# One 512-column product for both halves of the activations in the q, k and z projections

## The chip, the cores and the metric

The kernel runs on one core of a Trainium2 chip. The metric is the time of one execution on the device in microseconds (us); lower is better. TensorE (PE) multiplies, ScalarE (ACT) and VectorE (DVE) work on what it returns and on the weights, SyncE's queue (SP) issues nearly all loads.

## What is computed

Two decoder layers on 256 tokens of width 2048, in float32. Each layer normalises, scales and shifts its input, projects it, runs an attention, gates with silu(z), projects back and adds to the residual. Layer A has a dilated mixer with three patterns, so its projection makes ten parts of 2048 columns (q, k and v three times, and z); layer B has block attention and four parts (q, k, v, z). A last norm follows.

```
for i in range(DEPTH):                                    # DEPTH = 2
    mod = cond @ mod_w[i] + mod_b[i]
    shift, scale, gate = jnp.split(mod[:, None, :], 3, axis=-1)
    h = rms_norm(x, norm_w[i]) * (1.0 + scale) + shift
    if i % N_MIXERS == 0:
        y = dilated_mixer(h, a_w_in[j], slopes) @ a_w_out[j]
    else:
        y = moba_mixer(h, b_w_in[j], slopes) @ b_w_out[j]
    x = x + gate * y
return rms_norm(x, final_norm_w)
```

## The kernel before

**Split operands.** Every float32 operand of the big products is split into a high part that float32r holds exactly and a low part, the rest. A product is three passes: high by high, low by high, high by low. The activations lie split in SBUF as `hA` (layer A) and `hB` (layer B), tiles of 128 rows, 16 chunks, 2 halves (high, low) and 256 tokens, so the two halves of one chunk lie side by side, 512 columns in all.

**Units of weights.** A unit is 256 rows by 512 columns of a weight matrix, 512 KB. `convert` (L353) asks SP for its load into one of five buffers `raw`, and ACT copies it to the high part `wh` (L362); `finish_converts` (L366) lets DVE make the low part `wl` (L369). There are four buffers of `wh` and `wl` (`NB`, a ring); eight units held for longer use others.

**Parts and steps.** The sixteen heads are worked in four groups `j` of four heads. A part is one of q, k, v, z for one group: 8 units, 512 columns. Weights of v parts move past standing activations (`moving`, L303, products of 512 columns into two accumulators of 128 tokens). For q, k and z the weights stand and activations move (`stationary`, L315): for a head and a chunk of 128 rows three products of 256 columns, `wh` by high, `wh` by low, `wl` by high, all into the same 256 columns. Two heads share one PSUM bank, so a part takes two of the four accumulators `acc`, and the next part takes the other two. `evac` (L551) copies the finished banks to SBUF on ACT, with Silu for z.

**Order.** The order is written out by hand. A step is the products of one unit; `steps` lists them. `at_once(i, f)` puts work right after step i's products and ahead of the splitting of the next weights; `at(i, f)` puts it behind. `plan_conversions` (L372) lets a unit be loaded and split after the step in which the unit four places ahead in the ring was last used, and not over 8 steps ahead. Each engine works through its own instructions in that order.

**Stages.** Layer A begins with group 0 and six parts of group 1 (v0, v1, v2, z, q0, k0) in five strips of rows, since the modulation's scale and shift come strip by strip; each strip's products are added to what the earlier ones left (`evac_partial`, L542, on DVE). The last strip is one unit wide: 16 steps. Then come q1, k1, q2, k2 of group 1, all ten parts of group 2 and of group 3, the output projection, layer B's four groups (v, z, q, k), its output projection and the last norm. The attention of a group runs as items (`item_a`, one head and half the queries, 8 in a group; `item_b`, one head, 4 in a group), whose four stages are hung on later steps with given offsets: scores, normalising, transposes, output. Group 0's items begin at steps i0, i0 + 1, ... of group 1's q1, where i0 is the first step behind the strips. `add_piece` spreads loads of the modulation's weights and DVE's multiply-adds on them (L136) evenly over the steps of layer A behind the strips, and over layer B's groups 1 and 2.

Of the kernel before, what the change touches and what calls it, by code (L numbers as in the profile page):

```python
# [11 lines left out]
F32 = mybir.dt.float32  # L12
# [5 lines left out]
P = 128  # L18
# [13 lines left out]
def distance_masks():  # L32
    """-(t_q - t_k) where a key is seen, MASKED elsewhere, in blocks of 128 queries by 128 keys.

    The first six blocks: tokens of one parity each; the last three: tokens of one half each.
    """
    m = np.arange(P)

    def block(tq, tk, rule):
        d = tq[:, None] - tk[None, :]  # L40
        return np.where(rule(d), -d.astype(np.float32), np.float32(MASKED)).astype(np.float32)

    near = lambda d: (d >= 0) & (d <= 128)
    every = lambda n: (lambda d: (d >= 0) & (d % n == 0))
    even, odd, low, high = 2 * m, 2 * m + 1, m, m + P
    cols = [block(even, even, near), block(even, odd, near), block(even, even, every(4)), block(even, even, every(16)),
            block(odd, even, near), block(odd, odd, near)]
    cols += [block(q, k, lambda d: d >= 0) for q, k in ((low, low), (high, low), (high, high))]
    return np.ascontiguousarray(np.concatenate(cols, axis=1))
# [3 lines left out]
def trunk_kernel(ctx: ExitStack, tc: tile.TileContext, x, c, norm_w, mod_w, mod_b, a_w_in, a_w_out,  # L53
# [25 lines left out]

# [1 line left out]
    xnT = [ypool.tile([P, 8, S], F32, name=f"xnT{i}", tag=f"y{i}") for i in range(2)]  # L81
# [36 lines left out]

# [1 line left out]
    slots = {}  # L120

    def slot(i, name, dtype=F32):
        """A new tile in slot i, 0 .. 15."""
        if i < 12:
            return actp.tile([P, 1024], dtype, name=name, tag=f"a{i}")
        y = 2 + (i - 12) // 2
        if i % 2 == 0:
            slots[y] = ypool.tile([P, 2048], F32, name=f"ext{y}", tag=f"y{y}")
        return slots[y][:, (i % 2) * 1024:(i % 2 + 1) * 1024]

# [1 line left out]
    def mac(acc, raw, kc, first):  # L132
# [12 lines left out]
    def start_unit(u):  # L145
        """Strip 0: four chunks of rows of scale (u < 4) or shift; part of shift on the tensor engine."""
        part, i = 1 - u // 4, u % 4
        raw = rawp.tile([P, 4, 256], F32, name="raw", tag="raw")
        src = mod_w[0, i * 512:(i + 1) * 512, part * D:part * D + 256]
        nc.sync.dma_start(raw, src.rearrange("(c p) n -> p c n", p=P))  # L150
        for k in range(4):
            kc = 4 * i + k
            if u < 4 or 4 <= kc < 14:
                mac(start_acc[:, part * 256:(part + 1) * 256], raw[:, k], kc, (u, k) in ((0, 0), (5, 0)))
                continue
            for b in range(2):
                nc.tensor.matmul(start_ps[:, b:b + 1], raw[:, k, b * P:(b + 1) * P], ccT[:, kc:kc + 1],
                                 start=u == 4 and k == 0 and b == 0, stop=False, skip_group_check=True)
# [6 lines left out]
    def strip_unit(s, u):  # L165
        """Loads 1024 weights a partition of strip s of layer 0's shift (first half of the units) or scale."""
        w = 256 * STRIPS[s]
        n = 1024 // w
        part, i = divmod(u, KC // n)
        if u == 0:  # L170
            strip_acc[s] = maccp.tile([P, 1024], F32, name="macc", tag="macc")
        raw = rawp.tile([P, n, w], F32, name="raw", tag="raw")
        n0 = part * D + sum(STRIPS[:s]) * 256
        nc.sync.dma_start(raw, mod_w[0, i * n * P:(i + 1) * n * P, n0:n0 + w].rearrange("(c p) n -> p c n", p=P))
        for k in range(n):
            mac(strip_acc[s][:, part * w:(part + 1) * w], raw[:, k], i * n + k, i == 0 and k == 0)
# [13 lines left out]
    def column_sums(sums, acc, g, pool, tag):  # L190
        """sums[:, g] := sums over the rows of acc's columns 512 g .., 128 to a column."""
        pc = pool.tile([P, 512], F32, name="pcs", tag=tag)
        for b in range(4):
            nc.tensor.transpose(pc[:, b * P:(b + 1) * P], acc[:, (4 * g + b) * P:(4 * g + b + 1) * P], ident)
        nc.vector.tensor_reduce(sums[:, 4 * g:4 * g + 4], pc.rearrange("p (b k) -> p b k", b=4), axis=AX.X, op=ALU.add)
# [39 lines left out]

# [1 line left out]
    def rstd_of(ss, n):  # L237
        """(ss / D + EPS) ** -0.5"""
        r = small.tile([P, 2], F32, name="rstd")
        nc.gpsimd.tensor_scalar(r[:, :n], ss, 1.0 / D, EPS, op0=ALU.mult, op1=ALU.add)  # L240
        nc.gpsimd.tensor_tensor(r[:, :n], r[:, :n], nhalf[:, :n], op=ALU.pow)
        return r

    def split(dst, src):
        """dst[p, k, 0 / 1, t] := high and low part of src[p, k, t]."""
        hi = dst[:, :, 0]
        nc.scalar.activation(hi, src, AF.Copy)
        nc.vector.tensor_tensor(dst[:, :, 1], src, hi.bitcast(F32), op=ALU.subtract)
# [52 lines left out]

# [1 line left out]
    def moving(ps, st, kcs, w, tts, first, last):  # L303
        """ps[token, tile, n] += st.T @ w, for two chunks of rows of w."""
        wh, wl = w
# [9 lines left out]
    def stationary(ps, st, kcs, w, first, last):  # L315
        """ps[n, head, token] += w.T @ st"""
        wh, wl = w
# [9 lines left out]

# [1 line left out]
    units, steps, tasks, first_tasks, conv = [], [], {}, {}, {}  # L329
# [5 lines left out]

    def add_step(n, pe):
        i = len(steps)
        steps.append((n, pe))
        if units[n]["first"] is None:
            units[n]["first"] = i  # L340
        units[n]["last"] = i
        return i
# [4 lines left out]
    def at_once(i, f, *a):  # L347
        """As at, but ahead of the splitting of the next weights."""
        first_tasks.setdefault(i, []).append((f, a))
# [3 lines left out]
    def convert(n):  # L353
        """Loads a unit and makes its high parts; finish_converts() the low ones."""
        raw = rawp.tile([P, 2, GC], F32, name="raw", tag="raw")
# [16 lines left out]
    def plan_conversions():  # L372
        """After which step each unit is loaded and split: its tiles are free then."""
        ring, held, e, plan = [], {}, -1, {}
# [17 lines left out]

# [1 line left out]
    act = {}  # L394
# [18 lines left out]
    def bias_exp(ps, dmc, slope, parts, t):  # L413
        """t := exp of scaled scores with their bias, less the rows' maxima, in parts of columns; their sums."""
        n, w = len(parts), parts[-1].stop
# [24 lines left out]
    def item_a(j, hh, tt, base, offsets):  # L440
        """One head and one tile of queries of the dilated mixer."""
        st = {}
# [37 lines left out]
    def item_b(j, hh, base, offsets):  # L480
        """One head of the block mixer (one block): the queries of the first half see its keys, the others all."""
        st = {}
# [30 lines left out]

# [1 line left out]
    PARTS = ["v0", "v1", "v2", "z", "q0", "k0", "q1", "k1", "q2", "k2"]  # L515
# [17 lines left out]
    def product(p, key, st, n, u, first, last):  # L533
        def pe():
# [3 lines left out]
            else:  # L538
                moving(group_ps(key), st, kcs, conv[n], (0, 1), first, last)
        return add_step(n, pe)  # L540

    def evac_partial(key, s):  # L542
# [38 lines left out]
    for j in range(1, 4):  # L581
        i0 = len(steps)
        for i in range(8):
            base = i0 + i if j == 1 else i0 + 1 + 2 * i
            item_a(j - 1, i // 2, i % 2, base, (0, 1, 2, 4) if j == 1 else (0, 1, 3, 5))
        for n, p in enumerate(PARTS[EARLY:] if j == 1 else PARTS):
            for u in range(8):
                m = add_unit(wA, u, COL[p] * D + j * GC)
                i = product(p, ("A", j, p), st_a, m, u, u == 0, u == 7)
            at_once(i + 6 if j == 1 and n == 0 else i, evac, "A", j, p)  # L590

# [6 lines left out]

# [1 line left out]
    def out_steps(l, w, epilogue, hold):  # L600
# [102 lines left out]

# [1 line left out]
    st_b = lambda kc: hB_box[0][:, kc]  # L705
    for j in range(4):
# [4 lines left out]
        for p in PARTS_B:  # L711
            col = COL_B[p] * D + j * GC
            if j == 0 and p == "v":
                ns = [add_unit(wB, u, col, HOLD[u] if u < 4 else None)
                      for u in range(8)]
                for tt in range(2):
                    for u, n in enumerate(ns):
                        def pe(n=n, u=u, tt=tt, key=("B", j, p)):
                            moving(group_ps(key), st_b, (2 * u, 2 * u + 1), conv[n], (tt,), u == 0, u == 7)
                        i = add_step(n, pe)  # L720
            else:
                for u in range(8):
# [40 lines left out]

# [1 line left out]
    plan = plan_conversions()  # L765
# [55 lines left out]
```

## Time and profile before

| what | value |
|---|---|
| median of 3 runs | 1614.94 us (1614.93 to 1617.24) |
| span of the profiled execution | 1612.8 us |
| time of the profiled execution | not given apart from its span; the median is 2.1 us above the span |
| TensorE busy | 1579.9 us, 98% |
| TensorE weight loads busy | 1478.9 us, 92% |
| DVE busy | 1136.5 us, 70% |
| ACT busy | 743.6 us, 46% |

The span runs from the first to the last instruction that the profile shows. Products are pipelined and their ends are modelled, so TensorE's busy share says little of how much of its time is needed; weight loads run beside the products.

### The profile page before, as it was taken

To read this page: it belongs to the slowest core of one execution; us is meant where nothing else is said; L and a number is where in the kernel's file an instruction comes from. 1 tells how busy PE (TensorE), PEld (TensorE's weight loads), DVE (VectorE), ACT (ScalarE), POOL (GpSimd) and SP (SyncE) were. 2 spreads that over 40 slices of the span, in tenths; PEclk is the share of its full clock that TensorE was granted. 3 is DMA by queue.
4 is the path that set the end of the run, shared out by engine and by line. 5 is a ranking of instruction groups with operands and counts; after the bars stand their busy time and mean duration, and the time that the engine had idled before them with its cause. 6 is when DMAs were issued, how large, how long until landed. Compare 5 with 4: busy or idle time off the path is not lost.

```text
span 1612.8 us, 27220 instructions
## 1 busy us (share of the span) xinstructions
PE 1579.9 (98%) x10975; PEld 1478.9 (92%) x10975; DVE 1136.5 (70%) x1477; ACT 743.6 (46%) x971; POOL 12.1 (1%) x29
## 2 busy tenths in 40 slices
PE   5999999999999999999999999999999999999997
PEld 4999999999999889999889999887998999989986
DVE  6899899888756876666876665766446767664565
ACT  4643434334544544444544443554445445454543
POOL 0000000000000000000000000000000000000000
PEclk9999999999999999999999999999999999999999
DMA  9988797766468779888778887466467787856553
GB/s 310 322 280 293 247 322 263 253 208 185 133 205 272 230 238 298 282 285 278 232 261 286 280 287 233 126 210 211 133 183 237 253 267 239 278 166 202 172 170 119
DMA packets 182253, 380.97 MB, mean 236 GB/s; under 512 B 11616, under 2 KB 19952, under 8 KB 181616
## 3 DMA queue, kind: packets, MB, share of 16 engines
q1 hardware_dynamic: 180352, 373.93, 71.6%
q0 software_dynamic: 1008, 4.19, 0.7%
q8 instruction: 86, 1.41, 0.3%
q10 hardware_dynamic: 768, 1.12, 0.2%
q14 instruction: 39, 0.32, 0.1%
HBM read 377.10 MB, written 2.10 MB: 235 GB/s over the span
## 4 chain that ended last, share of the span: by engine, by line
PE 94%; DMA 2%; DVE 2%; ACT 1%; issue 1%; POOL 0%; POOLq 0%; DVEq 0%; ACTq 0%
PE acc L326 18%; PE acc L325 18%; PE acc L324 18%; PE acc L311 11%; PE acc L313 10%; PE acc L312 10%; PE po L472 2%; PE pss L454 2%; DMA raw<-in_mod_w_dram 2%; PE pst L435 1%; PE po L505 1%; PE pss L489 1%; DVE macc L136 1%; DMA raw<-in_a_w_in_dram 1%; ACT wh L362 0%
## 5 line engine op out<-in xcount | busy, mean ns | idle before, releaser
L362 ACT ACTIVATE wh<-raw 128x1024 fp32r<-128x1024 f32 x504 | 533.1, 1059 | 672.6 <-PE acc L325 396.3
L369 DVE TENSOR_TENSOR wl<-raw,wh 128x1024 fp32r<-128x1024 f32 (+1 forms) x505 | 612.8, 1220 | 261.5 <-ACT wh L362 260.3
L324 PE MATMUL acc<-hA,wh 128*128 128x256 f32 x1792 | 509.4, 284 | 0.0
L326 PE MATMUL acc<-hA,wl 128*128 128x256 f32 x1792 | 507.1, 283 | 0.0
L325 PE MATMUL acc<-hA,wh 128*128 128x256 f32 x1792 | 507.0, 283 | 0.0
L325 PEld LDWEIGHTS acc<-hA,wh 128*128 128x128 f32 x1792 | 343.9, 192 | 0.7
L324 PEld LDWEIGHTS acc<-hA,wh 128*128 128x128 f32 x1792 | 343.8, 192 | 0.7
L326 PEld LDWEIGHTS acc<-hA,wl 128*128 128x128 f32 x1792 | 343.8, 192 | 0.0
L136 DVE SCALAR_TENSOR_TENSOR macc<-raw,ccT,macc 128x1024 f32<-128x1024 f32 (+2 forms) x264 | 247.2, 936 | 22.8 <-DMA raw<-in_mod_w_dram 19.1
L324 PE MATMUL acc<-hB,wh 128*128 128x256 f32 x768 | 219.8, 286 | 0.0
L326 PE MATMUL acc<-hB,wl 128*128 128x256 f32 x768 | 217.4, 283 | 0.0
L325 PE MATMUL acc<-hB,wh 128*128 128x256 f32 x768 | 217.3, 283 | 0.0
L311 PE MATMUL acc<-wh,hA 128*128 128x512 f32 x384 | 155.4, 405 | 3.7 <-ACT actA1v L547 1.4
L312 PE MATMUL acc<-wl,hA 128*128 128x512 f32 x384 | 151.0, 393 | 0.3 <-DVE wl L369 0.3
L313 PE MATMUL acc<-wh,hA 128*128 128x512 f32 x384 | 150.8, 393 | 0.0
L324 PEld LDWEIGHTS acc<-hB,wh 128*128 128x128 f32 x768 | 147.3, 192 | 0.3
L325 PEld LDWEIGHTS acc<-hB,wh 128*128 128x128 f32 x768 | 147.3, 192 | 0.3
L326 PEld LDWEIGHTS acc<-hB,wl 128*128 128x128 f32 x768 | 147.2, 192 | 0.0
L311 PEld LDWEIGHTS acc<-wh,hA 128*128 128x128 f32 x384 | 72.9, 190 | 18.5 <-ACT actA1v L547 1.7
L313 PEld LDWEIGHTS acc<-wh,hA 128*128 128x128 f32 x384 | 72.6, 189 | 15.8
L312 PEld LDWEIGHTS acc<-wl,hA 128*128 128x128 f32 x384 | 72.8, 190 | 14.9 <-DVE wl L369 0.8
L422 ACT ACTIVATE t<-t,nm 128x512 f32<-128x512 f32 (+1 forms) x64 | 37.6, 587 | 58.9 <-DVE nm L420 58.7
(206 smaller groups left out, 1505.1 us busy)
## 6 DMA issues: line engine op xcount, KB each, us to landing
raw<-in_a_w_in_dram SPq DMA_DIRECT2D x320, 512.0 KB, 4.8
raw<-in_mod_w_dram SPq DMA_DIRECT2D x192, 512.0 KB, 4.6
raw<-in_b_w_in_dram SPq DMA_DIRECT2D x128, 512.0 KB, 4.5
raw<-in_a_w_out_dram SPq DMA_DIRECT2D x32, 512.0 KB, 3.8
raw<-in_b_w_out_dram SPq DMA_DIRECT2D x32, 512.0 KB, 3.8
xin<-in_x_dram SPq DMA_DIRECT2D x2, 1024.0 KB, 9.2
x<-in_x_dram POOLq DMA_DIRECT2D x4, 512.0 KB, 5.9
gate<-in_mod_b_dram SPq DMA_DIRECT2D x1, 1024.0 KB, 7.7
```

Of the source, the lines that this page charges most:

```text
L136: nc.vector.scalar_tensor_tensor(acc, raw, ccT[:, kc:kc + 1], acc, op0=ALU.mult, op1=ALU.add)
L311: nc.tensor.matmul(o, hi, wh[:, i], start=f, stop=False, skip_group_check=True)
L312: nc.tensor.matmul(o, hi, wl[:, i], start=False, stop=False, skip_group_check=True)
L313: nc.tensor.matmul(o, lo, wh[:, i], start=False, stop=l, skip_group_check=True)
L324: nc.tensor.matmul(o, wh[:, i, wc], hi, start=f, stop=False, skip_group_check=True)
L325: nc.tensor.matmul(o, wh[:, i, wc], lo, start=False, stop=False, skip_group_check=True)
L326: nc.tensor.matmul(o, wl[:, i, wc], hi, start=False, stop=l, skip_group_check=True)
L362: nc.scalar.activation(wh, raw, AF.Copy)
L369: nc.vector.tensor_tensor(wl[:, c], raw[:, c], wh[:, c].bitcast(F32), op=ALU.subtract)
L422: nc.scalar.activation(t[:, c], t[:, c], AF.Exp, bias=nm[:, i:i + 1], scale=SCALE, accum_out=l[:, i:i + 1])
L454: nc.tensor.matmul(ps[:, n:n + w], heads_of("A", j, f"q{g}")[:, hh, tok], heads_of("A", j, f"k{g}")[:, hh, ks], start=True, stop=True)
L472: nc.tensor.matmul(po[:, 0:P], vv, st["pT"][:, n], start=n == 0, stop=n == 3)
```

## The change

Thirty parts (q, k, z of layer A outside the strips, and of layer B) are made by a new function, `whole_part`. For a head and a chunk of 128 rows there are two products: `wh` by both halves of the activations side by side, 512 columns into a whole PSUM bank, and `wl` by the high half, 256 columns added to the first half of that bank. A head now has a bank of its own, and a part takes all four accumulators. When a head is done, ACT copies its second half (low activations) to SBUF and DVE adds the first half; z gets its Silu in place, once for the part, behind the last head.

A part now has 12 steps: units 0 and 1 together, head by head (4 steps); units 2, 3, 4, 5 for all heads (4 steps); units 6 and 7 together, head by head (4 steps, each followed by that head's copy and addition). A step may therefore use two units. Group 0's items start five steps earlier (i0 - 5 instead of i0), in the last strip; the later evacuation of q1 at step i + 6 goes. Parts in strips and v parts stay as they were. Lines with docstrings and comments are dropped as well.

```
+    def stationary_head(ps, st, kcs, w, h, first, last):
+        wh, wl = w
+        wc = slice(h * P, (h + 1) * P)
+        for i, kc in enumerate(kcs):
+            both = st(kc).rearrange("p a t -> p (a t)")
+            nc.tensor.matmul(ps, wh[:, i, wc], both, start=first and i == 0, stop=False, skip_group_check=True)
+            nc.tensor.matmul(ps[:, 0:S], wl[:, i, wc], both[:, 0:S], start=False, stop=last and i == len(kcs) - 1,
+                             skip_group_check=True)
...
-    def add_step(n, pe):
+    def add_step(ns, pe):
         i = len(steps)
-        steps.append((n, pe))
-        if units[n]["first"] is None:
-            units[n]["first"] = i
-        units[n]["last"] = i
+        steps.append((ns, pe))
+        for n in ns if isinstance(ns, tuple) else (ns,):
+            if units[n]["first"] is None:
+                units[n]["first"] = i
+            units[n]["last"] = i
         return i
...
+    def head_ps(key, h):
+        return groups.setdefault((key, h), None) or groups.update(
+            {(key, h): ps_acc.tile([P, GC], F32, name="acc", tag="acc")}) or groups[key, h]
...
+    def whole_part(l, j, p, st, w, col):
+        key = (l, j, p)
+        ns = [add_unit(w, u, col) for u in range(8)]
+
+        def pe(us, hs):
+            for h in hs:
+                for u in us:
+                    stationary_head(head_ps(key, h), st, (2 * u, 2 * u + 1), conv[ns[u]], h, u == 0, u == 7)
+
+        def evac_head(h):
+            ps = groups[key, h]
+            dst = act_of(l, j, p)[:, h * S:(h + 1) * S]
+            nc.scalar.activation(dst, ps[:, S:2 * S], AF.Copy)
+            nc.vector.tensor_tensor(dst, dst, ps[:, 0:S], op=ALU.add)
+            if p[0] == "z" and h == 3:
+                nc.scalar.activation(act[l, j, p], act[l, j, p], AF.Silu)
+
+        for us in ((0, 1), (2,), (3,), (4,), (5,), (6, 7)):
+            for hs in [(h,) for h in range(4)] if len(us) == 2 else [range(4)]:
+                i = add_step(tuple(ns[u] for u in us), lambda us=us, hs=hs: pe(us, hs))
+                if us[-1] == 7:
+                    at_once(i, evac_head, hs[0])
+        return i
...
-            base = i0 + i if j == 1 else i0 + 1 + 2 * i
+            base = i0 - 5 + i if j == 1 else i0 + 1 + 2 * i
             item_a(j - 1, i // 2, i % 2, base, (0, 1, 2, 4) if j == 1 else (0, 1, 3, 5))
         for n, p in enumerate(PARTS[EARLY:] if j == 1 else PARTS):
+            if p[0] != "v":
+                whole_part("A", j, p, st_a, wA, COL[p] * D + j * GC)
+                continue
             for u in range(8):
                 m = add_unit(wA, u, COL[p] * D + j * GC)
                 i = product(p, ("A", j, p), st_a, m, u, u == 0, u == 7)
-            at_once(i + 6 if j == 1 and n == 0 else i, evac, "A", j, p)
+            at_once(i, evac, "A", j, p)
...
+            elif p != "v":
+                i = whole_part("B", j, p, st_b, wB, col)
+                continue
             else:
                 for u in range(8):
                     i = product(p, ("B", j, p), st_b, add_unit(wB, u, col), u, u == 0, u == 7)
```

## Rows read from the trace of the kernel before

**Rows 1.** The page: span, busy time by engine, granted clock in 40 slices (tenths)
```profile
span 1612.8 us, 27220 instructions
...
PE 1579.9 (98%) x10975; PEld 1478.9 (92%) x10975; DVE 1136.5 (70%) x1477; ACT 743.6 (46%) x971; POOL 12.1 (1%) x29
...
PEclk9999999999999999999999999999999999999999
```

**Rows 2.** The chain of waits, its shares by engine and line
```profile
PE 94%; DMA 2%; DVE 2%; ACT 1%; issue 1%; POOL 0%; POOLq 0%; DVEq 0%; ACTq 0%
PE acc L326 18%; PE acc L325 18%; PE acc L324 18%; PE acc L311 11%; PE acc L313 10%; PE acc L312 10%; PE po L472 2%; PE pss L454 2%; DMA raw<-in_mod_w_dram 2%; PE pst L435 1%; PE po L505 1%; PE pss L489 1%; DVE macc L136 1%; DMA raw<-in_a_w_in_dram 1%; ACT wh L362 0%
```

**Rows 3.** Groups of instructions by line and shape: count, busy us, mean ns
```profile
L324 PE MATMUL acc<-hA,wh 128*128 128x256 f32 x1792 | 509.4, 284 | 0.0
...
L311 PE MATMUL acc<-wh,hA 128*128 128x512 f32 x384 | 155.4, 405 | 3.7 <-ACT actA1v L547 1.4 <-ACT hA L296 1.2 <-ACT ext L547 0.7
```

**Rows 4.** Order of time on PE, group 2's k2: first and last of 32
```profile
752.78 0.28 PE L324 MATMUL acc<-hA,wh 128*128 128x256 f32 x1
...
756.50 0.28 PE L325 MATMUL acc<-hA,wh 128*128 128x256 f32 x1
```

**Rows 5.** Order of time on PE, group 2's v2: first and last of 28
```profile
589.79 0.39 PE L311 MATMUL acc<-wh,hA 128*128 128x512 f32 x1
...
595.91 0.39 PE L311 MATMUL acc<-wh,hA 128*128 128x512 f32 x1
```

**Rows 6.** Busy time by window: group 2's parts z to k2
```profile
core 0: us, PE busy (x) PEld busy (x) DVE busy (x) ACT busy (x) POOL busy (x), PEclk, DMA share, GB/s
596.60:759.60 163.00, 163.00 (x1357) 162.82 (x1356) 110.06 (x97) 69.22 (x73) 0.00 (x0) 1.00 0.87 288
```

**Rows 7.** TensorE's own waits: us in total, times, longest (first four of eleven)
```profile
PE pxt L273 <- ACT xin L267: 9.7, 1, 9.7
PE pst L106 <- ACT t L104: 4.5, 1, 4.5
PE pxt L273 <- DVE xin L265: 3.0, 1, 3.0
PE acc L311 <- ACT actA1v L547: 1.4, 1, 1.4
```

**Rows 8.** Groups by line and shape on ACT, then on DVE
```profile
L362 ACT ACTIVATE wh<-raw 128x1024 fp32r<-128x1024 f32 x504 | 533.1, 1059 | 672.6 <-PE acc L325 396.3 <-PE acc L313 117.3 <-DMA raw<-in_a_w_in_dram 79.9
...
L554 ACT ACT_TABLE_LOAD x6 | 7.7, 1283 | 0.1
...
L554 ACT ACTIVATE actA2q<-acc 128x512 f32<-128x512 f32 x6 | 3.6, 597 | 4.0 <-PE acc L326 4.0
...
L247 ACT ACTIVATE yB<-ysb 128x256 fp32r<-128x256 f32 x16 | 6.7, 418 | 3.6 <-DVE ysb L508 2.6
...
L557 ACT ACTIVATE actA0z<-actA0z 128x1024 f32<-128x1024 f32 x1 | 1.0, 1042 | 0.0
...
L369 DVE TENSOR_TENSOR wl<-raw,wh 128x1024 fp32r<-128x1024 f32 x503 | 611.5, 1222 | 261.5 <-ACT wh L362 260.3
L136 DVE SCALAR_TENSOR_TENSOR macc<-raw,ccT,macc 128x1024 f32<-128x1024 f32 x120 | 153.5, 1279 | 2.0 <-DMA raw<-in_mod_w_dram 2.0
...
L508 DVE TENSOR_TENSOR ysb<-po,actB0z 128x256 f32<-128x256 f32 x4 | 1.7, 424 | 4.2 <-PE po L505 4.2
```

**Rows 9.** Waits of all engines, then of the load queue (SP)
```profile
ACT wh L362 <- PE acc L325: 396.3, 228, 2.3
...
ACT wh L362 <- DMA raw<-in_a_w_in_dram: 79.9, 42, 3.7
...
SPq L356 <- DVE wl L369: 625.7, 300, 18.3
```

**Rows 10.** Loads by line: count, KB each, median us from issue to landing
```profile
raw<-in_a_w_in_dram SPq DMA_DIRECT2D x320, 512.0 KB, 4.8
```

**Rows 11.** Order of time on DVE, one step of the last strip
```profile
388.99 1.22 DVE L369 TENSOR_TENSOR wl<-raw,wh 128x1024 fp32r<-128x1024 f32 x1
390.12 0.68 DVE L549 TENSOR_TENSOR actA1v<-actA1v,acc 128x512 f32<-128x512 f32 x1
391.10 0.69 DVE L549 TENSOR_TENSOR actA1v<-actA1v,acc 128x512 f32<-128x512 f32 x1 [0.30 <-PE acc L313]
391.70 1.22 DVE L369 TENSOR_TENSOR wl<-raw,wh 128x1024 fp32r<-128x1024 f32 x1
```

**Rows 12.** Order of time on DVE, one step with stages of items
```profile
422.09 0.29 DVE L474 TENSOR_TENSOR ysb<-po,actA0z 128x128 f32<-128x128 f32 x1 [1.01 <-PE po L472]
422.77 0.29 DVE L248 TENSOR_TENSOR yA<-ysb,yA 128x128 fp32r<-128x128 f32 x1 [0.39 <-ACT yA L247]
422.98 0.15 DVE L428 RECIPROCAL rl<-l 128x1 f32<-128x1 f32 x1
423.17 0.49 DVE L430 TENSOR_SCALAR t<-t,rl 128x512 f32<-128x512 f32 x1
423.57 0.68 DVE L417 SCALAR_TENSOR_TENSOR t<-dm,pss 128x512 f32<-128x512 f32 x1
424.29 0.69 DVE L419 TENSOR_REDUCE m<-t 128x1 f32<-128x512 f32 x1
425.01 0.15 DVE L420 TENSOR_SCALAR nm<-m 128x1 f32<-128x1 f32 x1
425.08 1.22 DVE L369 TENSOR_TENSOR wl<-raw,wh 128x1024 fp32r<-128x1024 f32 x1
```

**Rows 13.** Order of time on PE, that step's products of items
```profile
421.00 1.05 PE L472 MATMUL po<-pT,actA0v 128*128 128x128 f32 x8
421.89 0.60 PE L435 MATMUL pst<-ident,t 128*128 128x128 f32 x4
422.33 1.04 PE L454 MATMUL pss<-actA0k,actA0q 128*128 128x256 f32 x6
423.13 0.36 PE L324 MATMUL acc<-hA,wh 128*128 128x256 f32 x1
```

**Rows 14.** Busy time by window with DMA share and GB/s; the page's GB/s by slice
```profile
600.00:640.00 40.00, 40.00 (x335) 40.00 (x335) 27.17 (x23) 16.93 (x18) 0.00 (x0) 1.00 0.90 298
...
GB/s 310 322 280 293 247 322 263 253 208 185 133 205 272 230 238 298 282 285 278 232 261 286 280 287 233 126 210 211 133 183 237 253 267 239 278 166 202 172 170 119
```


## The prediction

> **What bounds the kernel now.** I read the page first: the span is 1612.8 us, TensorE is busy in 98% of it, at a granted clock of 9 tenths or more in every slice [rows 1]. A busy share alone proves nothing, since the ends of pipelined products are modelled, so I went to the chain of waits: 94% of it is TensorE, about 55% the three lines of `stationary` and 31% those of `moving` [rows 2]. Third, TensorE's own waits: the longest three are 9.7, 4.5 and 3.0 us, at the start, the next is 1.4, and all eleven come to 23 us [rows 7]. So the kernel is a queue of products run back to back. An edit pays by the time that products take from start to start, and costs only where it makes TensorE wait.
>
> That time I took from the order of time, not from the mean durations (284 ns and 405 ns [rows 3] overlap). With 256 columns 32 products in a row start from 752.78 to 756.50: 3.72 us over 31 gaps, **120.0 ns** each [rows 4]. With 512 columns 28 products start from 589.79 to 595.91: 6.12 over 27, **226.7 ns** [rows 5]. So 256 more columns cost 106.7 ns, and a product has a fixed part of 120.0 - 106.7 = **13.3 ns** that does not depend on its width. In both streams each product has its own weight load, as in the new order.
>
> A check on a whole stretch: the seven parts z to k2 of group 2 run from 596.6 to 759.6, 163.0 us with 1357 products [rows 6]. 7 x 64 triples of 3 x 120.0 ns are 161.3 us; the other dozen, small products of the modulation, fill the rest. Nothing else is hidden there.
>
> **What the change removes and adds on TensorE.** Old, for a head and 128 rows of weights: three products of 256 columns, 3 x 120.0 = 360.0 ns. New: one of 512 and one of 256, 226.7 + 120.0 = 346.7 ns. Saved: 13.3 ns, one product's fixed part with its weight load. How often: `whole_part` makes 4 parts of group 1, 7 of group 2, 7 of group 3 and 3 of each of the four groups of layer B: 4 + 14 + 12 = 30 parts of 64. The ten others stay in strips on `stationary`. 30 x 64 = 1920 times 13.3 ns = **25.6 us**. The mixed order itself is in no row. A bound above: the new product of 256 follows one of 512, under which its load has time to spare; but in the stream of 512 the load is as well covered and the 13.3 ns remain, so I allow no more gain. A bound below: the pair costs as much as the three, and nothing is saved. I take 25.6, since both widths give the same fixed part.
>
> Here a rule speaks against the change. The Trainium skill, TensorE: Matmul & The Clock Gate, section "Wait — 56ns, not 53.3ns?", gives a warm product N / 2.4 GHz plus about 2.5 ns; the granted clock here is 1.00, the level of 2.4 GHz [rows 6], yet the fixed part by rows is 13.3 ns. By the Trainium skill's figure, as an estimate, 1920 x 2.5 ns = 4.8 us would be all that is saved.
>
> **Evacuation.** Old: two ACT copies of 512, 0.60 us each, for a part. New, for each of four heads: an ACT copy of 256 columns (nearest row, 256 columns within SBUF, 0.42 us) and a DVE addition of 256 that reads PSUM (like the ysb product, 0.42 us) [rows 8]. For 30 parts that is 120 x 0.42 = 50 us of DVE, and 50 in place of 36 us of ACT. DVE is busy 70% of the span, ACT 46% [rows 1], neither sets the end, so the work itself is free as long as it keeps its dates.
>
> **Dates at the seam of two parts.** A part now fills all four accumulators, so the next one's head 0 needs head 0's back. That head ends three steps of 4 x 346.7 ns = 1.39 us ahead of the seam: 4.2 us for copy and addition, under 1 us with their hops. Covered.
>
> The ring of four split weights is tighter: units 6 and 7 of one part and 0 and 1 of the next hold all of it until the last head's step. Take the seam as time 0. Unit 2 is wanted after four steps, at 5.55 us, its low part at 5.8. ACT: last head's copy to 0.5, high part of unit 2 (1.06) to 1.6, of unit 3 to 2.7 [rows 8]. DVE: addition to 1.0, a multiply-add of the modulation (1.28) to 2.3, low part of unit 2 (1.22) to 3.5: 2.3 us ahead. Units 4 and 5 come free at 5.55 and are wanted at 11.1 and 13.9. This asks that the loads have landed: one takes 4.8 us [rows 10], but ACT's splitting waited for TensorE's buffers 396 us and for loads 80 us in all, and the load queue waits for DVE's release of its five buffers (626 us), so loads run ahead [rows 9]. I take no wait.
>
> After z, Silu in place (1.04) and a table load (1.28) [rows 8] stand ahead of unit 2's split: 0.5 + 1.28 + 1.04 + 1.06 + 1.22 plus hops is about 5.3 us against 5.8. Six such z parts, 0 to 1 us each; with half a microsecond in hand I take **1 us** in all.
>
> **The moved attention items.** Group 0's eight items start five steps earlier, in the last strip, whose DVE is nearly full: a step lasts 2.71 us there, 2.41 of it DVE's (0.30 idle) [rows 11]. An item takes 0.29 + 0.29 + 0.15 + 0.49 + 0.68 + 0.69 + 0.15 = 2.74 us of DVE and a wait of 0.39 in its queue [rows 12], and 2.13 us of TensorE (421.00 to 423.13) [rows 13]. Together 5.5 us of DVE against 2.7 + 2.1 = 4.8 of TensorE: DVE falls behind by up to 0.7 us a step, 3.5 us over five steps, then perhaps 1 us more over the short steps of q1 (1.39 + 2.13 against 3.7). The splits queued behind it have three units of lead, some 10 us, so most of it is hidden. Bounds 0 and 4.5 us; I take **2 us**. The items' own work on TensorE is the same, only earlier.
>
> **The rest.** Load and multiply-add of the modulation now come every 2.5 steps instead of 1.75 (192 to 264 steps), with shorter steps: every 4.6 us instead of 5.0 in these parts. The later gate loads, the residual's loads and the output projection keep their places and have no waits to lose.
>
> **Sum.** -25.6 + 1 + 2 = -22.6 us. The profiled execution's span is 1612.8; its own time isn't given, and the median of the runs is 1614.94, 2.1 above the span. I forecast a span near 1590 and a median of **1592.3 us**.
>
> **Rivals.**
> - *The loads become the bound in the whole parts.* A part takes 64 x 346.7 ns = 22.2 us, in which eight units and 4.8 of the modulation's loads arrive: 12.8 x 0.524 MB = 6.7 MB, 302 GB/s. The old stretch moved 298 with the DMA engines 90% busy [rows 14]. If 298 were the ceiling, a part would take 22.5 us; over the 24 parts with such loads, 0.3 us each, 7 us go: 1599. Against it: the second slice shows 322 GB/s [rows 14]. Uneven bursts at the seams would show alike.
> - *The seam stalls, and the kernel is slower.* If unit 2's load were only issued as the seam comes, its low part would be ready at 4.8 + 1.06 + 1.22 + 0.3 = 7.4 us, 1.6 late, 30 times: 48 us against 22.6, 1640. It decides from 22.6 / 30 = 0.75 us a part. Against it are [rows 9].
> - *The fixed part doesn't go*, because 13.3 ns is no cost of a product and the pair takes nearly 360 ns: nothing is saved, and up to 3 us of delays remain: 1615 to 1618, no change that a measurement tells. For it speaks only that the mixed order isn't shown. The Trainium skill's 2.5 ns (TensorE: Matmul & The Clock Gate) would end near here too, by estimate at 1614.9 - 4.8 + 3 = 1613.
> - *More is saved*, the 256-wide product's fixed part also vanishing under the wide one: another 25.6 us, 1567. The stream of 512 speaks against it.
>
> **Numbers.** Forecast 0.70 (1589 to 1595, all delays from none to 5.5 us), loads 0.16, stalled seams 0.07, nothing saved 0.04, more saved 0.03. The range takes in the forecast and nearly all of the case of the loads: 1588 to 1604. About 0.2% (3.2 us) is what a measurement of this kernel can tell from no change: faster 0.89, same 0.04, slower 0.07.
>
> **What the profile after would show.** Right: 1920 products fewer; in the parts z to k2 starts alternate by about 227 and 120 ns, and seven parts take 155 to 157 us instead of 163; no new wait of TensorE above a few us in total. Wrong: a gap after 512 columns of 240 (nothing saved) or 213 (more); waits of the new wide product for wh, wl or the additions, once a part (seam); ACT's splitting waiting for loads in these parts (loads); low parts late around the end of the last strip (items).

## The result and the profile after

| what | before | after |
|---|---|---|
| median | 1615.29 us (4 runs) | 1603.63 us (4 runs, 1602.65 to 1604.31) |
| ratio | | 0.9926, interval [0.9912, 0.9941] |
| span of the profiled execution | 1612.8 us | 1600.8 us (its own time 1602.65) |

The kernel is 11.7 us faster; 22.6 were forecast. The time lies in the range, 0.4 us below its upper end. So half of the gain is missing, and the question is where. The page after, in the order of [rows 1] and [rows 2]:

```profile
span 1600.8 us, 23586 instructions
...
PE 1566.6 (98%) x9055; PEld 1376.3 (86%) x9055; DVE 1173.7 (73%) x1597; ACT 756.9 (47%) x1039; POOL 12.0 (1%) x29
...
PEclk9999999999999999999999999999999999999999
...
PE 92%; DVE 3%; DMA 3%; ACT 2%; issue 1%; POOL 0%; POOLq 0%; DVEq 0%; ACTq 0%
```

The 1920 products are gone (10975 to 9055), the clock is the same, and TensorE still sets the end. Waits did not take the gain: TensorE's own waits come to 25 us in all, where they came to 23 [rows 7]. The longest three, and the two that are new:

```profile
PE pxt L273 <- ACT xin L267: 9.4, 1, 9.4
PE pst L106 <- ACT t L104: 4.7, 1, 4.7
PE pxt L273 <- DVE xin L265: 2.5, 1, 2.5
...
PE pst L451 <- DVE t L446: 1.3, 3, 0.7
...
PE pst L451 <- ACT pT L453: 0.3, 1, 0.3
```

No wide product waits for a split weight or for an evacuation; the new waits are 1.6 us, those of the moved items' transposes. What is left is the time between starts. The order of time on TensorE from group 2's q0 into k0 (the first two products, and the one that starts 12 pairs later):

```profile
639.65 0.40 PE L335 MATMUL acc<-hA,wh 128*128 128x512 f32 x1
639.88 0.28 PE L336 MATMUL acc<-hA,wl 128*128 128x256 f32 x1
...
643.89 0.40 PE L335 MATMUL acc<-hA,wh 128*128 128x512 f32 x1
```

4.24 us over 12 pairs are **353.3 ns**, where 346.7 were forecast from [rows 4] and [rows 5]. Further on, in q2, two starts 23 pairs apart:

```profile
717.81 0.39 PE L335 MATMUL acc<-hA,wh 128*128 128x512 f32 x1
...
725.78 0.40 PE L335 MATMUL acc<-hA,wh 128*128 128x512 f32 x1
```

7.97 over 23 are **346.5 ns**. The same two lines of code run at two rates, each steady over hundreds of products. Between these two places the change falls on two foreign products (products of other work that stand between the pairs), the modulation's, of 512 columns:

```profile
653.43 0.40 PE L335 MATMUL acc<-hA,wh 128*128 128x512 f32 x1
653.66 0.28 PE L336 MATMUL acc<-hA,wl 128*128 128x256 f32 x1
653.78 0.63 PE L207 MATMUL psy<-t,ones_r 128*128 128x512 f32 x2
654.25 0.39 PE L335 MATMUL acc<-hA,wh 128*128 128x512 f32 x1
654.47 0.28 PE L336 MATMUL acc<-hA,wl 128*128 128x256 f32 x1
```

Ahead of it a pair takes 353.3 ns, behind it 346.7. Worked out from all starts of the trace, with the delayed ones left out: 235.7 ns behind a wide product and 116.6 behind a narrow one, 352.2 a pair in the mean; about five pairs in six run at the slow rate. 1920 x (360.0 - 352.2) = 15 us saved in place of 25.6.

### The profile page after: what moved, and what is told of

It is laid out like the page before. It is cut to its first block, busy times and chain, and to the rows that moved or that the text cites. A ratio compares the mean times of both kernels' runs of the same rounds, so it can differ in the third digit from the quotient of the medians.

```text
span 1600.8 us, 23586 instructions
## 1 busy us (share of the span) xinstructions
PE 1566.6 (98%) x9055; PEld 1376.3 (86%) x9055; DVE 1173.7 (73%) x1597; ACT 756.9 (47%) x1039; POOL 12.0 (1%) x29
## 4 chain that ended last, share of the span: by engine, by line
PE 92%; DVE 3%; DMA 3%; ACT 2%; issue 1%; POOL 0%; POOLq 0%; DVEq 0%; ACTq 0%
PE acc L335 28%; PE acc L336 14%; PE acc L313 10%; PE acc L311 10%; PE acc L312 10%; PE acc L326 4%; PE acc L325 4%; PE acc L324 4%; DMA raw<-in_mod_w_dram 2%; PE pss L470 2%; PE po L488 1%; PE pst L451 1%; DVE macc L136 1%; PE po L521 1%; PE pss L505 1%
## 5 line engine op out<-in xcount | busy, mean ns | idle before, releaser
L335 PE MATMUL acc<-hA,wh 128*128 128x512 f32 x1152 | 407.8, 399 | 0.0
L335 PE MATMUL acc<-hB,wh 128*128 128x512 f32 x768 | 274.8, 401 | 0.0
L335 PEld LDWEIGHTS acc<-hA,wh 128*128 128x128 f32 x1152 | 216.4, 188 | 52.3
L336 PEld LDWEIGHTS acc<-hA,wl 128*128 128x128 f32 x1152 | 217.4, 189 | 0.2
L324 PE MATMUL acc<-hA,wh 128*128 128x256 f32 x640 | 182.1, 284 | 0.0
L325 PE MATMUL acc<-hA,wh 128*128 128x256 f32 x640 | 181.1, 283 | 0.0
L335 PEld LDWEIGHTS acc<-hB,wh 128*128 128x128 f32 x768 | 144.3, 188 | 34.6
L325 PEld LDWEIGHTS acc<-hA,wh 128*128 128x128 f32 x640 | 122.8, 192 | 0.4
L324 PEld LDWEIGHTS acc<-hA,wh 128*128 128x128 f32 x640 | 122.7, 192 | 0.4
L326 PEld LDWEIGHTS acc<-hA,wl 128*128 128x128 f32 x640 | 122.7, 192 | 0.0
```

Source lines behind the costliest of these rows:

```text
L324: nc.tensor.matmul(o, wh[:, i, wc], hi, start=f, stop=False, skip_group_check=True)
L325: nc.tensor.matmul(o, wh[:, i, wc], lo, start=False, stop=False, skip_group_check=True)
L326: nc.tensor.matmul(o, wl[:, i, wc], hi, start=False, stop=l, skip_group_check=True)
L335: nc.tensor.matmul(ps, wh[:, i, wc], both, start=first and i == 0, stop=False, skip_group_check=True)
L336: nc.tensor.matmul(ps[:, 0:S], wl[:, i, wc], both[:, 0:S], start=False, stop=last and i == len(kcs) - 1, skip_group_check=True)
```

## The experiments

Three theories: **A**, the products save less than forecast because alternating widths have a slow rate; **B**, they save it all and the seams give half back; within A, **A1**, each change of width has a price, **A2**, there are two steady rates and the way a stretch is entered chooses, **A3**, the place (buffers, the other engines' work) chooses.

**Three narrow products in the new order.** All of the change but the wide product:

```
-            nc.tensor.matmul(ps, wh[:, i, wc], both, ...)
-            nc.tensor.matmul(ps[:, 0:S], wl[:, i, wc], both[:, 0:S], ...)
+            nc.tensor.matmul(ps[:, 0:S], wh[:, i, wc], hi, ...)
+            nc.tensor.matmul(ps[:, S:2 * S], wh[:, i, wc], lo, ...)
+            nc.tensor.matmul(ps[:, 0:S], wl[:, i, wc], hi, ...)
```

> The new parts, steps, banks and evacuations, but three products of 256 columns as before (high by high into the first half of the bank, high by low into the second, low by high into the first). Theory A (the product's saving was smaller than forecast: the alternation of 512 and 256 columns takes 353.3 ns a pair in most stretches and 346.7 in some, 352.2 in the mean, where three narrow ones take 360): 1920 x (360 - 352.2) = 15 us slower than the changed kernel, 1618.6, so some 3 us slower than the kernel before, which is what the new seams and the moved items cost. Theory B (the products save the full 25.6 us and the seams eat half of it): 1603.6 + 25.6 = 1629. Starts 120 ns apart in either.

1618.38 us (10 runs), ratio to before 1.0018 [1.0008, 1.0027]; A had said 1618.6 and B 1629, so B falls. It is 14.75 us slower than the changed kernel (15.3 by that kernel's second run below): the products are worth 14.75 us / 1920 = 7.7 ns a pair, and the new schedule alone costs 1.3 to 4.4 us (2.5 by the medians). Starts are 120.0 ns apart (35 gaps):

```profile
639.72 0.28 PE L336 MATMUL acc<-hA,wh 128*128 128x256 f32 x1
...
643.92 0.28 PE L335 MATMUL acc<-hA,wh 128*128 128x256 f32 x1
```

**All wide.** `wl` by both halves as well (adds the low by low product to the sum):

```
-            nc.tensor.matmul(ps[:, 0:S], wl[:, i, wc], both[:, 0:S], ...)
+            nc.tensor.matmul(ps, wl[:, i, wc], both, ...)
```

> The low weights too are multiplied by both halves, 512 columns: a stream of 512 columns alone, with the activations moving. Theory A (only the alternation is slow): starts 226.7 ns apart as in the v parts, 453.3 a pair, 1603.6 + 1920 x 101 = 1798 us. Theory C (512 columns of activations are slow by themselves, 233 ns): 466.7 a pair, 1823 us.

1797.06 us (one run), 1798 expected. Starts 226.7 ns apart (4.76 us over 21 gaps), so 512 columns of activations in a long row are not slow by themselves. The mixture is:

```profile
699.64 0.39 PE L335 MATMUL acc<-hA,wh 128*128 128x512 f32 x1
...
704.40 0.39 PE L336 MATMUL acc<-hA,wl 128*128 128x512 f32 x1
```

**Two wide, then two narrow**, for each unit and head:

```
         for i, kc in enumerate(kcs):
             both = st(kc).rearrange("p a t -> p (a t)")
             nc.tensor.matmul(ps, wh[:, i, wc], both, ...)
+        for i, kc in enumerate(kcs):
             nc.tensor.matmul(ps[:, 0:S], wl[:, i, wc], st(kc)[:, 0, :], ...)
```

> For each unit and head the two products of 512 columns first, then the two of 256: half as many changes of width. Theory A1 (each change from wide to narrow costs 6.67 ns, and the 346.7 ns stretches are another matter): the four take 700 instead of 706.7 ns, 960 x 6.67 = 6.4 us faster than the changed kernel, 1597. Theory A2 (alternation has two steady rates, and which one holds is set by how the stretch was entered): no fixed price for a change of width; the four take 693.3 where no slow rate exists in this order, 1603.6 - 1920 x 5.5 ns = 1593, or 706.7 where it does, 1603.6; seen by the four starts being constant over a stretch and different between stretches.

1596.24 us, ratio 0.9877 [0.9862, 0.9891]: 7.4 us faster than the changed kernel. The time lies 0.8 us from A1's 1597, but the trace has neither theory's rate: the four take 696.7 ns in every long stretch (939.68 to 945.95, nine fours, 6.27 us), halfway between A2's 693.3 and A1's 700. There is one rate, not two:

```profile
939.68 0.62 PE L335 MATMUL acc<-hA,wh 128*128 128x512 f32 x2
940.14 0.40 PE L337 MATMUL acc<-hA,wl 128*128 128x256 f32 x2
...
945.95 0.40 PE L335 MATMUL acc<-hA,wh 128*128 128x512 f32 x1
```

**Narrow first**, and the same once more:

```
-            nc.tensor.matmul(ps, wh[:, i, wc], both, start=first and i == 0, stop=False, ...)
+            nc.tensor.matmul(ps[:, 0:S], wl[:, i, wc], both[:, 0:S], start=first and i == 0, stop=False, ...)
-            nc.tensor.matmul(ps[:, 0:S], wl[:, i, wc], both[:, 0:S], start=False, stop=last and i == len(kcs) - 1, ...)
+            nc.tensor.matmul(ps, wh[:, i, wc], both, start=False, stop=last and i == len(kcs) - 1, ...)
```

> In each pair the product of 256 columns (low weights) ahead of the one of 512. The alternation is the same, only the entry into a stretch differs. Theory A1 (a price for each change of width): the same 352 to 353 ns a pair, 1603.6. Theory A2 (two steady rates, set by the entry): the stretches that were at 353.3 can come out at 346.7 and the other way; if all were at 346.7, 1593; some stretches must change their rate against the changed kernel.

1597.43 us, ratio 0.9885 [0.987, 0.99]; the second time 1597.68 (1597.4 expected). Nearly all long stretches are now at 346.7 ns; z of group 2 up to the first foreign products (160 pairs) and group 0 of layer B (192 pairs) stay at 353.4, both entered straight from a v part. A1 falls: as many changes of width, another time.

**Longer blocks**: in each step all wide products, then all narrow ones (4 and 4, or 8 and 8).

```
...
+            for wide in (True, False):
                 for h in hs:
                     for u in us:
-                        stationary_head(..., u == 0, u == 7)
+                        stationary_head(..., u == 0, u == 7, wide)
```

> In each step all products of 512 columns first, then all of 256: blocks of 4 and 4 in the steps of one head, of 8 and 8 in those of one unit, in place of 2 and 2. In the run with 2 and 2 the four took 696.7 ns everywhere, 3.3 more than 2 x 346.7. If that is a price for each change of width and back: blocks of 4 take 1390, blocks of 8 take 2777 ns, or 347.3 ns a pair in the mean, 1.0 ns x 1920 = 2 us faster than 2 and 2, 1594.3. If a narrow or a wide product takes longer whatever stands before it: 348.3 a pair, 1596.2. Low parts are wanted later in a step, so no new waits.

1598.43 us, where 1594.3 or 1596.2 were expected. A block of 8 and 8 takes 2790 ns (939.92 to 945.50 is two of them), 348.8 a pair and not 347.1. A block of 4 and 4 takes 1402 ns (953.91 to 959.52 is four), 350.6 a pair, where 1390 were expected:

```profile
939.92 2.00 PE L336 MATMUL acc<-hA,wh 128*128 128x512 f32 x8
...
942.71 2.00 PE L336 MATMUL acc<-hA,wh 128*128 128x512 f32 x8
...
945.50 0.86 PE L336 MATMUL acc<-hA,wh 128*128 128x512 f32 x3
...
953.91 1.09 PE L336 MATMUL acc<-hA,wh 128*128 128x512 f32 x4
...
959.52 0.86 PE L336 MATMUL acc<-hA,wh 128*128 128x512 f32 x3
```

A part has eight blocks of 4 and four of 8, 22.38 us against 22.29 in two and two; over 30 parts that is 2.5 us, about the 2.2 between the two medians. So there is no fixed price for a change of width that longer blocks would thin out.

**Kicks in the changed kernel.** Two extra products into a bank that nobody reads, ahead of four parts:

```
+            if (l, j, p) in KICKED and us[0] == 0 and list(hs) == [0]:
+                pk = ps_y.tile([P, 512], F32, name="psy", tag="y")
+                for n in range(2):
+                    nc.tensor.matmul(pk, ones_r, st(0).rearrange("p a t -> p (a t)"), ...)
```

> The changed kernel, with two extra products of 512 columns (into a spare bank that nobody reads) ahead of four parts that lay within slow stretches: q0 of group 2, q2 of group 3, and q of groups 0 and 3 of layer B. In the changed kernel the rate went from 353.3 to 346.7 ns behind two such products at 653.8 us. Theory A2 (two steady rates, chosen by the entry): behind at least some of the four the rate turns to 346.7 ns and stays until the next foreign products, where without them it stayed at 353.3; up to 250 pairs behind the four, less the other stretches, 1 to 3 us gained against 4 x 0.47 = 1.9 us for the kicks: 1601 to 1604. Theory A3 (the rate belongs to the place, the buffers or the other engines' work at that time): 353.3 behind all four, 1603.6 + 1.9 = 1605.5.

1604.95 us (one run): outside A2's 1601 to 1604 and nearer A3's 1605.5, so the time alone speaks against A2. The trace shows why. Behind two of the four kicks the rate turns to 346.7 ns and stays so for 96 and 128 pairs; behind the other two it stays 353.3; and the 192 pairs from 663.94, at 346.7 in the changed kernel, go to 353.4. In all some 100 more pairs run at the lower time, 0.7 us, against 1.9 for the kicks. The first kick:

```profile
620.92 0.40 PE L335 MATMUL acc<-hA,wh 128*128 128x512 f32 x1
...
621.98 0.40 PE L335 MATMUL acc<-hA,wh 128*128 128x512 f32 x1
622.22 0.28 PE L336 MATMUL acc<-hA,wl 128*128 128x256 f32 x1
622.33 0.63 PE L568 MATMUL psy<-hA,ones_r 128*128 128x512 f32 x2
...
623.03 0.28 PE L336 MATMUL acc<-hA,wl 128*128 128x256 f32 x1
...
629.97 0.28 PE L336 MATMUL acc<-hA,wl 128*128 128x256 f32 x1
```

Three pairs in 1.06 us ahead of it (353.3), twenty in 6.94 behind it (347). In the changed kernel run once more the same place stays slow, twenty pairs in 7.07 us (353.5):

```profile
621.88 0.28 PE L336 MATMUL acc<-hA,wl 128*128 128x256 f32 x1
...
628.95 0.28 PE L336 MATMUL acc<-hA,wl 128*128 128x256 f32 x1
```

> The changed kernel itself, on the same chip as the three orders beside it: 1603.6, its rates as before (about five pairs in six at 353.3 ns), if what sets them is in the program and not in the run.

1603.08 us, the rates in the long stretches as in its first profile. So the place and its buffers do not choose by themselves, as A3 has it: the same place takes either rate.

**Kicks with the narrow product first**, ahead of its two slow stretches, first with two products of 512 columns as above, then with four small ones in their place:

```
...
+                for n in range(4):
+                    nc.tensor.transpose(pk[:, n * P:(n + 1) * P], ident, ident)
```

> The order with the narrow product first, with two extra products of 512 columns ahead of z of group 2 and z of layer B's group 0, the two long stretches that were at 353.4 ns in it (160 and 192 pairs, both entered from a v part). Theory A2: both at 346.7, 352 x 6.7 ns = 2.3 us gained less 2 x 0.47 for the kicks, 1.4 us: 1596.0. Theory A3 (the place decides): both stay at 353.4, 1598.4.

1597.63 us: a miss for A2, both stretches stay at 353.4 ns, as A3 had it. A reading made afterwards: the kick was of 512 columns like the v products ahead of it, so the entry was of the same kind. The next run tests it.

> The order with the narrow product first, and ahead of z of group 2 and z of layer B's group 0 four transposes of 128 columns into a spare bank that nobody reads, in place of the two products of 512 columns that changed nothing there. In that order all long stretches that were entered from such small float32 products ran at 346.7 ns, those entered from products of 512 columns at 353.4. Theory A2 (the entry chooses the rate): both stretches turn to 346.7, (160 + 192) x 6.7 ns = 2.3 us gained against 2 x 0.45 for the transposes, 1.4 us faster than the order without them, 1596.0. Theory A3 (the place decides): both stay at 353.4, 1598.3.

> The order with the narrow product first, again, on the same chip: 1597.4, z to k2 of group 2 at 353.4 ns up to the first foreign products, layer B's group 0 at 353.4.

1595.85 us [0.9858, 0.9891], beside 1597.68 [0.9873, 0.9902] without it: the intervals overlap, and the trace decides. Both stretches turn to 346.7 ns. The entry, and 13 pairs in 4.51 us (346.9) behind it:

```profile
597.18 0.39 PE L313 MATMUL acc<-wh,hA 128*128 128x512 f32 x1
597.41 0.60 PE L568 MATMUL psy<-ident 128*128 128x128 f32 x4
597.76 0.36 PE L335 MATMUL acc<-hA,wl 128*128 128x256 f32 x1
...
598.32 0.39 PE L337 MATMUL acc<-hA,wh 128*128 128x512 f32 x1
...
602.83 0.39 PE L337 MATMUL acc<-hA,wh 128*128 128x512 f32 x1
```

Without the transposes, in the first run of that order, 14 pairs take 4.94 us there (352.9):

```profile
600.06 0.28 PE L335 MATMUL acc<-hA,wl 128*128 128x256 f32 x1
...
605.00 0.28 PE L335 MATMUL acc<-hA,wl 128*128 128x256 f32 x1
```

Later stretches went slow in return: 192 pairs behind the modulation's products at 661 us, and the pairs from 890.87 to 917. In all some 230 more pairs run at 346.7 ns than in the run beside it, 1.5 us, against 0.9 for the transposes: the rates carry about 0.6 of the 1.8 us between the two medians. This kernel and two and two are the fastest seen, about 1596 us, and can't be told apart by time.

## Why the prediction was half right

**The step that failed** is the term "1920 times 13.3 ns = 25.6 us". The mechanism was right (a product has a fixed part, and taking products out saves it), the size was not: measured 14.75 us, 7.7 ns a pair. "The mixed order itself is in no row" was the weak point, and its bounds, nothing and 13.3, held the truth between them; I took the upper one because both pure streams gave it. That the time still lies in the range is luck: the range reached up to 1604 for the sake of the loads, and without them it ended at 1595. The kernel before had a warning that I passed over. [rows 5] is a settled stretch of wide products; elsewhere they were slower, as at the end of group 3's v2, 2.32 us over ten gaps, 232 ns:

```profile
841.73 0.40 PE L312 MATMUL acc<-wl,hA 128*128 128x512 f32 x1
...
844.05 0.39 PE L313 MATMUL acc<-wh,hA 128*128 128x512 f32 x1
```

A fixed part that is 13.3 ns in one place and 19 in another is no constant. The place tells which: in the v parts of groups 2 and 3, the second to ninth gaps of a stretch average 231 ns, those from the eleventh on 226.7, and the stretch shown is only twelve products long. In the mixed order every wide product stands behind one of another width; that the same thing slows both is likely, but not shown. The check with [rows 6] was made on narrow products alone and couldn't show it.

**Delays, 3 us forecast.** The schedule alone costs 2.5 us by the medians of the first experiment. The *items*, 2 us: from the last strip's j = 1 parts (385.43) to group 2's v0 (511.99) took 126.56 us before; with three narrow products in the new order, where the products are equal, 387.43 to 516.48 is 129.05. These are 2.5 us, mostly at the items' transposes. TensorE is idle 1.4 us ahead of them, most of it waiting for DVE's normalising, where the kernel before shows none:

```profile
L452 PE MATMUL pst<-ident,t 128*128 128x128 f32 x32 | 4.9, 277 | 1.4 <-DVE t L447 0.9 <-ACT pT L454 0.3
```

The *seams and z parts*, 1 us: no wait is seen, and group 2's parts z to k2 take 163.03 us with three narrow products, as before.

**Rivals.** The loads did not become the bound: in the parts z to k2 the engines moved 295 GB/s at a share of 0.88, and ACT's splitting waited for layer A's loads 109 us where it had waited 80 [rows 9], but no wait for a split weight shows on a TensorE product there. The wait, and the window (busy time of PE, PEld, DVE, ACT and POOL, granted clock, DMA share, GB/s):

```profile
ACT wh L374 <- DMA raw<-in_a_w_in_dram: 109.3, 62, 3.8
...
597.26:755.92 158.66, 158.66 (x909) 138.22 (x908) 118.40 (x124) 70.78 (x87) 0.00 (x0) 1.00 0.88 295
```

The time came out between the 1599 that the rival of the loads gave and the 1604 that the range allowed it, for another reason. The stalled seams did not come. "The fixed part doesn't go" was true by half; its sign, a gap of 240 behind a wide product, showed in a part of the gaps (233, 236 and 241 ns in turn). Seven parts took 158.7 us, above the 155 to 157 named. By the Trainium skill (TensorE: Matmul & The Clock Gate, section "Wait — 56ns, not 53.3ns?") the saving would have been 4.8 us by estimate; 14.75 were measured, so the measurement decides against its figure too.

## What to carry to other kernels

A start-to-start time taken from a stream of equal products is not the price of that product in a mixed order: time the order itself, over several stretches, ahead of trusting a saving of a few per cent. Where products of two widths alternate, try the other order, and two and two: the same products came out 6 to 7 us faster here, with no other change. And run the new schedule with the old products: one kernel split the result into 14.75 us of gain and 2.5 of cost.

## What was not expected of the hardware

Alternating products of 512 and 256 columns, each with its weight load, run on at 346.7 or 353.3 ns a pair, at a granted clock of 1.00. In these runs the rate of a long stretch mostly stays as it was entered; foreign products can change it, and in four profiles it changed within a stretch too (near 890 us three times, at 677 once), with no foreign product there. The one at 677 is in the second run of the narrow-first kernel; in its first run the same 192 pairs stay at 346.7 ns to the end, so the program alone does not settle the rate. Two and two has one rate, 348.3. What inside TensorE locks it is not settled: no run separates the weight load from the product, and why a given entry leads to a given rate stays open: two products of 512 columns ahead of the wide-first order turned it at some places and not at others.
